# Two-layer trunk: another order of the value products, another place for the norm's products, and two-map buffers with a later combine in attention

## The chip, the cores and the metric

The kernel runs on one core of a Trainium2 chip. The metric is the device time of one execution in microseconds (us); lower is better. The core has a matrix engine (TensorE, PE in the profile, with its weight loads as PEld), VectorE (DVE), ScalarE (ACT), GpSimd (POOL), and a queue of DMA issues (SP). Each engine takes its instructions in a fixed order and waits for semaphores of the others.

## The reference, cut to what matters

The program has two layers over 1024 tokens of width 1024, in fp32. The first layer mixes tokens by a gated MLP and a gated delta rule, the second by differential attention; each layer then has an MLP and a gate with a second input ("PLE"). The change touches the second layer's value projection and attention:

```python
hn = rms_norm(h, ln_mix_o[i])
q, k, v = jnp.split(hn @ w_qkv_o[i], 3, axis=-1)
# 8 heads, two maps of 64 each; v: 8 heads of 128
q = rms_norm(q, q_gain) * 64 ** -0.5
k = rms_norm(k, k_gain)
logits = q @ k.T - slopes * dist          # for both maps, causal
probs = softmax(logits)
attn = probs[:, :, 0] - lam * probs[:, :, 1]
o = attn @ v
o = rms_norm(o, sub_gain) * (1.0 - lam_init)
```

with `rms_norm(h, g) = h * rsqrt(mean(h * h) + eps) * g` over the features of a token.

## The kernel before, in words

**Precision.** A matrix operand is held as a pair hi and lo of a reduced fp32 format, and a product of two operands is three passes of PE (`mm3`: hi·hi, hi·lo, lo·hi). `split` makes such a pair: a cast on ACT (L231) gives hi, a subtraction on DVE or POOL (L235) gives lo. Weights come from memory by DMA through a ring of raw tiles and a ring of split tiles (`w`).

**Hidden state.** `h` lies with features on the partitions, in two halves of 512 tokens: `acc[m][half]` is features 128m onward. `put_h` (L246, L247) makes the pair hi, lo of h times the norm's gain. The factor r, one over the root of the mean square of a token, is applied to a product's result and not to its operand. `add_square` (L258) sums the squares of a half into `sqs`, 128x512; `rms` adds those over the partitions with four 128x1 products against a column of ones (the trace counts them as eight), scales on DVE (L274), and takes the power on POOL (L276).

**The PLE gate** (`ple`) runs over the two halves. At the end of each half it calls `put_h` for its eight tiles, then `take_hs`, which calls `rms`. The last thing in it is therefore the second half's `rms`.

**The value projection** (`values`) comes next. It multiplies two by two blocks of 512 (a: tokens half and feature half; b: feature half and value column half) by a scheme of seven block products in place of eight, with sums of blocks as operands: s1 to s4 of tokens, t1 to t4 of weights. One block product (`product`) is 4 k-tiles by 4 banks by 3 passes = 48 passes of 128x512. There are two sets of four PSUM banks, x and y. The order in the text is a11·b11 into x, a12·b21 into y, s2·t2 into x (added to what is there), s1·t1 into y (new), s3·t3 into x, s4·b22 into y, a22·t4 into x. `copies` (ACT) takes a set out to SBUF, scaled by r; `close` takes a set out to the result, scaled and added to an earlier copy on DVE (L765), and without such a copy on ACT; `store` writes it to `v_dram`. The sums of tokens s1 to s4 overwrite `acc` (L738, L740).

**Attention** follows. It has 8 heads of 8 blocks of 128 queries. For a block, `logits(r)` of map r = 0, 1 multiplies q by the keys (two passes, qh and ql), DVE adds the bias and takes a running minimum (L1234), ACT takes the exponential with its sum (L1237). `combine` (L1243 to L1245) adds the second map, times a factor from both sums, to the first. `transpose` turns the combined block on PE and copies it out on ACT (L1255), `value` multiplies it by v (`po`, L1265). At step g the loop issues logits(0) of block g, the combine of g-1, the transpose of g-2, logits(1) of g and the value of g-2. `lg0` has three buffers in turn (two in A4, one in A5), `lg1` has one (the rest of A5).

Beside these steps `pump` feeds PE with the projections of q and k of the next head (256-wide passes), whose results leave by L1143 to L1152: a square on ACT, a reduction on DVE (L1145), an addition and a power on POOL (L1146, L1148), and two multiplications on DVE (L1152). `begin` turns k and q of the next head, with their copies on ACT and DVE (L1188, L1189 for `ks`; L1200 to L1202 for `qh` and `ql`), in the step of block 6, or 7 for the last; the second half of the keys follows at block 2 or 3. v is read from `v_dram` for two heads at a time, 1 MB each, into A0 and A1 in turn: two reads at the start, the others at steps 18 and 34.

**What sets the order.** A scheduler with a timeline of its own orders each engine's instructions. The class `Ordered` lets the program pin PE instructions behind others (`behind`, and `floor`, which holds all that follows behind a given product). PE's instructions carry L81 (products) and L84 (transposes). The lines named here and in the prediction are the kernel before's, unless it says otherwise; from L717 on the changed file's numbers differ by a few.

Of the kernel before, what the change touches and what calls it, by code (L numbers as in the profile page):

```python
# [18 lines left out]
P = 128  # L19
# [100 lines left out]
class Trunk:  # L120
# [144 lines left out]
    def rms(self, half, sqs, ms=None, rows=True, far=False):  # L265


        nc = self.nc
        if ms is None:
            pt = self.aux_ps()  # L270
            for t in range(4):
                self.pe.matmul(pt[:, t : t + 1], lhsT=sqs[:, t * P : (t + 1) * P], rhs=self.ones[:, 0:1], start=True, stop=True)
            ms = self.sp.tile([P, 4], F32, tag="ms", name=self.nm("ms"))
            nc.vector.tensor_scalar(ms, pt[:, 0:4], 1.0 / D, EPS, ALU.mult, ALU.add)  # L274
        r = self.sp.tile([P, 4], F32, tag=f"r{half}", name=self.nm("r"))
        nc.gpsimd.tensor_tensor(r, ms, self.mhalf[:, 0:4], ALU.pow)  # L276
# [12 lines left out]
        return r, rb  # L289
# [372 lines left out]
    def ple(self, pT, acc, wg, wpj, gain_next, h_dram):  # L662
# [19 lines left out]
        for h in range(2):  # L682
# [18 lines left out]
            self.take_hs(h, rows=False)  # L701

    def values(self, acc, gain, w_qkv):
# [7 lines left out]
        def tt(out, a, b, op):  # L713
            nc.vector.tensor_tensor(out, a, b, op)
            return out
# [42 lines left out]
        def close(i, l, ps, plus=None):  # L758
            for q in R:
                t = self.tmp()  # L760
                f = r[i][:, q : q + 1]
                if plus is None:
                    nc.scalar.activation(t, ps[q], AF.Copy, scale=f)
                else:
                    nc.vector.scalar_tensor_tensor(t, ps[q], f, plus[q], ALU.mult, ALU.add)  # L765
                store(i, l, q, t)

        b11 = right(lambda k: raw(0, 0, k))
        t1 = [self.slot(f"c{8 + k}", [P, HT], F32, "t1") for k in R]
        t2 = [self.slot(f"c{4 + k}", [P, HT], F32, "t2") for k in R]  # L770
        for k in R:
            tt(t1[k], raw(0, 1, k), raw(0, 0, k), ALU.subtract)
# [14 lines left out]
        s1, s2, s3, s4 = ([acc[m + k][h] for k in R] for m, h in ((4, 1), (0, 0), (0, 1), (4, 0)))  # L787
        for k in R:
            scaled(s3[k], k, 0, s3[k], ALU.subtract)
            scaled(s2[k], k, 0, s1[k], ALU.subtract)  # L790
        for k in R:
            scaled(s4[k], 4 + k, 0, s2[k], ALU.add)
        s2s = left(("A4", "A5"), s2)
        t2s = right(lambda k: t2[k])
# [3 lines left out]
        t1s = right(lambda k: t1[k])  # L798
        t = [self.slot(f"c{8 + k}", [P, HT], F32, "t") for k in R]
        product(y, s1s, t1s, True)  # L800
        copies(t, y, 1)

        def make_t3(k):
            b = raw(1, 1, k)
            return tt(b, b, raw(0, 1, k), ALU.subtract)
# [4 lines left out]
        close(1, 1, x, t)  # L810
        s4s = left(("A3", "A2"), s4)
# [288 lines left out]
    def attention(self, w_qkv, v_dram, w_out, gain_next, h_dram):  # L1100
# [107 lines left out]
        class Block:  # L1208


            def __init__(me, hd, b):
                me.hd, me.b, me.g = hd, b, len(blocks)
                me.n = (b + 1) * P
                me.lg = [lg0[len(blocks) % 3], lg1]
# [42 lines left out]
            def value(me):  # L1257
# [3 lines left out]
                o, v = os[hd], vs[hd // 2]  # L1261
                po = self.aux([P, P], "sc", "po")
                for k in range(b + 1):
                    self.pe.matmul(po, lhsT=me.aT[k // 4][:, (k % 4) * P : (k % 4 + 1) * P], rhs=v[:, k, (hd % 2) * P : (hd % 2 + 1) * P], start=k == 0, stop=k == b)
# [48 lines left out]
        qks, vs, os = [[] for _ in range(8)], [], [[] for _ in range(8)]  # L1313

        def values(pr):
            vs.append(self.slot(f"A{pr % 2}", [P, NT, 256], F32, "v"))
            nc.sync.dma_start(vs[pr], v_dram[:, :, pr * 256 : (pr + 1) * 256].rearrange("t p f -> p t f"))
# [41 lines left out]
        for g in range(8 * NB + 2):  # L1359
            if g in (2 * NB + 2, 4 * NB + 2):  # L1360
                values(g // (2 * NB) + 1)
# [4 lines left out]
            if 0 < g <= 8 * NB:  # L1366
                blocks[g - 1].combine()
# [978 lines left out]
```

## Time and profile before

| | |
|---|---|
| median of three runs | 2523.72 us (2525.03, 2522.82, 2523.72) |
| profiled execution | 2523.94 us, span 2522.2 us, granted clock 0.997 |
| up to 1188 us (first layer, up to the second half of its PLE gate) | PE busy 1185.57 of 1188.00 |
| 1188 to 1224, end of the gate and start of the value products | in the prediction |
| 1224 to 1291, the rest of the value products | PE busy 67.00 of 67.00, granted clock 0.98 |
| 1291 to 1308, projections ahead of the first head | PE busy 17.00 of 17.00 |
| 1308 to 1650, attention | in the prediction |
| 1650 to the end (output projection, MLP, gate) | PE busy 866.14 of 872.00 |

The granted clock is the share of full speed that PE was given. A row of the timeline has the start, the duration of one instruction or of the group from its first start to its last end, the engine, the line, out<-in and the count; in brackets stands the idle time of the engine before it and what ended that. A row of the waits has the waiting instruction, what released it, the sum in us, the count, and the longest.

### The profile page before, as it was taken

Reading aid. Unit: us, or ns where it says so; the run is one execution under the profiler, and the core shown is the slowest. Engines: PE = TensorE matmul, PEld = TensorE weight load, DVE = VectorE, ACT = ScalarE, POOL = GpSimd, SP = SyncE. Lnnn points to the kernel's source line nnn. Section 1 sums busy time; section 2 is a strip of 40 time slices with the busy share of each in tenths; the row PEclk is TensorE's granted clock in tenths of the full one; section 3 lists DMA queues with packets and bytes.
Section 4 is the critical chain, followed back from the end, with each engine's and each line's share of the span. In section 5 each row is a group of like instructions: output and inputs, shape, how many; then the busy total and the mean of one; then the engine's idle time right before and its main releaser. Section 6 shows DMA issues by size and latency. Waiting matters only on the chain.

```text
span 2522.2 us, 39013 instructions
## 1 busy us (share of the span) xinstructions
PE 2492.6 (99%) x13465; PEld 2114.7 (84%) x13465; DVE 1813.1 (72%) x3510; ACT 1346.0 (53%) x2732; POOL 245.6 (10%) x235
## 2 busy tenths in 40 slices
PE   9999999999999999999999999999999999999999
PEld 8898998888888888888799888988788888888887
DVE  7867664887666887556837777777887666787576
ACT  6635473655555445444536776765654555445452
POOL 0211220000000000000033433320000000000000
PEclk9999999999999999999999999999999999999999
DMA  8464445567558656554340211266467558656651
GB/s 240 126 181 112 149 127 164 163 207 250 177 172 281 216 179 201 180 159 139 117 142 27 68 43 59 89 205 223 149 214 240 178 177 282 209 185 203 198 174 65
DMA packets 322447, 420.46 MB, mean 167 GB/s; under 512 B 46692, under 2 KB 178760, under 8 KB 322248
## 3 DMA queue, kind: packets, MB, share of 16 engines
q1 hardware_dynamic: 321688, 417.43, 51.5%
q8 instruction: 106, 1.74, 0.3%
q14 instruction: 93, 0.76, 0.1%
q10 hardware_dynamic: 560, 0.53, 0.1%
HBM read 301.46 MB, written 116.40 MB: 166 GB/s over the span
## 4 chain that ended last, share of the span: by engine, by line
PE 92%; DVE 4%; ACT 2%; issue 1%; DMA 0%; POOL 0%; SPq 0%; DVEq 0%; ACTq 0%
PE mm L81 81%; PE po L81 2%; PE aux L81 2%; PE qk L81 2%; PE tr L84 2%; DVE lg L1234 1%; ACT lg L1237 1%; ACT qh L1201 0%; ACT qh L1200 0%; PE pks L81 0%; PE pkq L81 0%; PE pkk L81 0%; PE pvn L81 0%; PE pgm L81 0%; DVE w L235 0%
## 5 line engine op out<-in xcount | busy, mean ns | idle before, releaser
L231 ACT CAST w<-raw 128x512 fp32r<-128x512 f32 x582 | 357.2, 618 | 475.2 <-PE mm L81 431.9
L81 PE MATMUL mm<-g,w 128*128 128x512 f32 x2592 | 601.2, 394 | 0.0
L81 PEld LDWEIGHTS mm<-g,w 128*128 128x128 f32 x2592 | 486.7, 188 | 113.4
L81 PE MATMUL mm<-hi,w 128*128 128x512 f32 x1728 | 554.2, 395 | 0.0
L235 DVE TENSOR_TENSOR w<-raw,w 128x512 fp32r<-128x512 f32 (+1 forms) x550 | 376.0, 690 | 199.7 <-ACT w L231 191.3
L81 PE MATMUL mm<-w,hi 128*128 128x256 f32 (+2 forms) x2112 | 439.0, 303 | 4.8 <-DVE k L1152 4.8
L81 PEld LDWEIGHTS mm<-hi,w 128*128 128x128 f32 x1728 | 324.3, 188 | 74.0 <-DVE w L235 0.4
L81 PEld LDWEIGHTS mm<-w,hi 128*128 128x128 f32 x2112 | 338.4, 189 | 24.5 <-DVE k L1152 6.3
L81 PE MATMUL mm<-lo,w 128*128 128x512 f32 x864 | 340.2, 394 | 0.0
L81 PE MATMUL mm<-w,lo 128*128 128x256 f32 (+2 forms) x1056 | 317.4, 301 | 0.0
L81 PE MATMUL mm<-t,w 128*128 128x512 f32 x1152 | 271.5, 394 | 0.0
L81 PEld LDWEIGHTS mm<-t,w 128*128 128x128 f32 x1152 | 216.5, 188 | 50.7
L81 PEld LDWEIGHTS mm<-w,lo 128*128 128x128 f32 x1056 | 199.3, 189 | 8.0
L81 PEld LDWEIGHTS mm<-lo,w 128*128 128x128 f32 x864 | 162.4, 188 | 36.2
L276 POOL TENSOR_TENSOR r<-ms,mhalf 128x4 f32<-128x4 f32 x12 | 14.6, 1213 | 1554.3 <-DVE ms L274 1523.5
L235 DVE TENSOR_TENSOR g<-graw,g 128x512 fp32r<-128x512 f32 x216 | 147.7, 685 | 3.6 <-DMA gd<-g 3.5
L231 ACT CAST g<-graw 128x512 fp32r<-128x512 f32 x216 | 132.9, 618 | 19.4 <-DVE g L235 5.6
L1237 ACT ACTIVATE lg<-lg,nm 128x1024 f32<-128x1024 f32 (+7 forms) x128 | 99.5, 778 | 59.1 <-DVE nm L1234 58.6
L371 ACT ACTIVATE g<-g 128x512 f32<-128x512 f32 x100 | 63.1, 632 | 78.5 <-DVE g L305 78.1
L81 PE MATMUL mm<-ohi,w 128*128 128x512 f32 x256 | 85.0, 400 | 0.6 <-DVE acc L1452 0.3
L1234 DVE CUSTOM_DVE_ANT_0 lg<-qk,al 128x512 f32<-128x512 f32 (+3 forms) x128 | 74.1, 587 | 15.1 <-PE qk L81 12.0
L81 PE MATMUL mm<-ahi,w 128*128 128x512 f32 x256 | 83.1, 400 | 0.2 <-ACT ahi L1785 0.2
(373 smaller groups left out, 3673.4 us busy)
## 6 DMA issues: line engine op xcount, KB each, us to landing
raw<-in_w_mlp_dram SPq DMA_DIRECT2D x352, 256.0 KB, 3.2
graw<-gd SPq DMA_DIRECT2D x224, 256.0 KB, 2.7
gd<-g SPq DMA_DIRECT2D x192, 256.0 KB, 3.3
raw<-in_w_ple_gate_dram SPq DMA_DIRECT2D x76, 256.0 KB, 3.7
acc<-h_dram SPq DMA_DIRECT2D x64, 256.0 KB, 4.9
keep<-in_w_mlp_dram SPq DMA_DIRECT2D x64, 256.0 KB, 4.6
raw<-in_w_in_e_dram SPq DMA_DIRECT2D x60, 256.0 KB, 3.7
h_dram<-acc SPq DMA_DIRECT2D x48, 256.0 KB, 2.9
```

The lines of the kernel that those rows point to most:

```text
L81: self._next(self.engine.matmul(*a, **k))
L84: self._next(self.engine.transpose(*a, **k))
L231: inst = self.nc.scalar.copy(hi, src)
L235: inst = (lo_engine or self.nc.vector).tensor_tensor(lo, src, f32(hi), ALU.subtract)
L276: nc.gpsimd.tensor_tensor(r, ms, self.mhalf[:, 0:4], ALU.pow)
L371: nc.scalar.activation(g, src, AF.Relu)
L1234: nc.vector.tensor_tensor_reduce(out=lg[:, k0:k1], in0=ps[:, : k1 - k0], in1=al[:, u0 + k0 : u0 + k1], scale=-0.5 ** (hd + 1), scalar=3.0e ...
L1237: nc.scalar.activation(lg[:, :n], lg[:, :n], AF.Exp, bias=nm[:, r, nch - 1 : nch], scale=-1.0, accum_out=me.sums[:, b, r : r + 1])
```

## The change

**Value products.** The first product is now a12·b21, into y, copied out by ACT; the second a11·b11, into x, closed on DVE with that copy. Then come the second half's ones products of `rms`: `ple` calls `take_hs` for the first half only, `values` calls `rms` for the second with the bank `y[0]`, and `floor` holds its products behind the last product issued before it. The third product is a22·t4, which has no sum of tokens as operand; its result is copied to four tiles w. The four products with sums of tokens follow: s2·t2, s1·t1, s3·t3, s4·b22. s2 goes to tiles of its own (c0 to c3). All sixteen result tiles are closed on DVE; before, four of them were plain copies on ACT.

**Attention.** The three buffers each hold both maps (A4, A5, A1), so `lg1` turns through three as `lg0` does. The combine of block g-1 is issued after logits(1) of block g. With A1 taken, v has A0 alone, in two halves of 512 KB: a read for each head, at block 2 of the head before it (and two at the start).

```diff
-    def rms(self, half, sqs, ms=None, rows=True, far=False):
+    def rms(self, half, sqs, ms=None, rows=True, far=False, pt=None):
...
-            pt = self.aux_ps()
+            pt = self.aux_ps() if pt is None else pt
...
-            self.take_hs(h, rows=False)
-
+            if h == 0:
+                self.take_hs(0, rows=False)
+        self.hs[1] = self.hs_new[1]
...
-        b11 = right(lambda k: raw(0, 0, k))
+        b21 = right(lambda k: raw(1, 0, k))
...
-        product(x, a11, b11, True)
-        copies(u, x, 0)
-        b21 = right(lambda k: raw(1, 0, k))
-        for k in R:
-            tt(t2[k], t1[k], raw(1, 1, k), ALU.subtract)
-        product(y, a12, b21, True)
-        close(0, 0, y, u)
+        product(y, a12, b21, True)
+        copies(u, y, 0)
+        b11 = right(lambda k: raw(0, 0, k))
+        for k in R:
+            tt(t1[k], raw(1, 1, k), ALU.subtract, t2[k])
+        product(x, a11, b11, True)
+        close(0, 0, x, u)
+
+        self.pe.floor = self.pe.mark
+        r[1] = self.rms(1, self.sqs[1], rows=False, pt=y[0])[0]
+        self.pe.floor = None
...
+        t4s = right(lambda k: tt(raw(1, 0, k), t2[k]))
+        product(y, a22, t4s, True)
+        s2 = [scaled(self.slot(f"c{k}", [P, HT], F32, "s2"), k, 0, s1[k], ALU.subtract) for k in R]
+        s2s = left(("A4", "A5"), s2)
+        t2s = right(lambda k: t2[k])
...
+        copies(w, y, 1)
...
         product(x, s2s, t2s)
         copies(u, x, 0)
         s1s = left(("A0", "c"), s1)
         t1s = right(lambda k: t1[k])
+        product(y, s1s, t1s, True)
...
         close(1, 1, x, t)
+        close(1, 0, x, w)
         s4s = left(("A3", "A2"), s4)
         b22 = right(lambda k: raw(1, 1, k))
         product(y, s4s, b22)
         close(0, 1, y, u)
-        t4s = right(lambda k: tt(t2[k], t2[k], raw(1, 0, k), ALU.add))
-        product(x, a22, t4s)
-        close(1, 0, x)
...
-        lgs = [self.slot(f"A{4 + i}", [P, 2, S], F32, "lg") for i in range(2)]
-        lg0 = [lgs[0][:, 0], lgs[0][:, 1], lgs[1][:, 0]]
-        lg1 = lgs[1][:, 1]
+        lgs = [self.slot(t, [P, 2, S], F32, "lg") for t in ("A4", "A5", "A1")]
+        lg0, lg1 = ([x[:, r] for x in lgs] for r in range(2))
...
-                me.lg = [lg0[len(blocks) % 3], lg1]
+                me.lg = [lg0[len(blocks) % 3], lg1[len(blocks) % 3]]
...
-        def values(pr):
-            vs.append(self.slot(f"A{pr % 2}", [P, NT, 256], F32, "v"))
-            nc.sync.dma_start(vs[pr], v_dram[:, :, pr * 256 : (pr + 1) * 256].rearrange("t p f -> p t f"))
+        vs = self.slot("A0", [P, 2, NT, P], F32, "v")
+
+        def values(hd):
+            nc.sync.dma_start(vs[:, hd % 2], v_dram[:, :, hd * P : (hd + 1) * P].rearrange("t p f -> p t f"))
...
-            if g in (2 * NB + 2, 4 * NB + 2):
-                values(g // (2 * NB) + 1)
+            if g % NB == 2 and 0 < g // NB < 7:
+                values(g // NB + 1)
...
-            if 0 < g <= 8 * NB:
-                blocks[g - 1].combine()
             pump()
...
                 blocks[g].logits(1)
+            if 0 < g <= 8 * NB:
+                blocks[g - 1].combine()
             pump()
```

What stands where on an engine, before and after, at three places; the first is the seam between gate and value products, on two engines. In the rows a number behind a name tells one tile from another; an instruction that has a second row with 128x1 alone is the running minimum's write.

PE at the second half's ones products, first before (`mm` are the value products' banks, `w` the split weights, `hi` and `lo` the token operands, `aux` the ones' bank):

```order
L81 MATMUL mm_12293<-w_12352,lo_11737 128x512
L81 MATMUL mm_12293<-w_12358,hi_11740 128x512
L81 MATMUL mm_12293<-w_12359,hi_11740 128x512
L81 MATMUL mm_12293<-w_12358,lo_11741 128x512
L81 MATMUL aux_12224<-ones,sqs_11849 128x1 x4
L81 MATMUL mm_12287<-w_12236,hi_11720 128x512
L81 MATMUL mm_12287<-w_12237,hi_11720 128x512
```

The same place after (`mm_12281` is y's first bank, the one that the ones borrow; the other three of y and one of x are 12282 to 12284 and 12277; `s` is a part of s2):

```order
L81 MATMUL mm_12282<-w_12470,hi_12216 128x512
L81 MATMUL mm_12283<-w_12470,hi_12216 128x512
L81 MATMUL mm_12284<-w_12470,hi_12216 128x512
L81 MATMUL mm_12277<-w_12547,s_12537 128x512
L81 MATMUL mm_12281<-ones,sqs_11849 128x1 x4
L81 MATMUL mm_12282<-w_12471,hi_12216 128x512
L81 MATMUL mm_12282<-w_12470,lo_12217 128x512
```

Before, 54 of the value products stand ahead of the ones; after, 118 do, all of the first two block products and part of the third among them.

DVE at the last addition to `sqs`, before (`acc` are sums of tokens, `t` the PLE gate's, `s` and `w` lower parts of operands):

```order
L235 TENSOR_TENSOR s_12467<-acc_8285,s_12466 128x512
L740 SCALAR_TENSOR_TENSOR acc_8288<-acc_8288,cols,acc_8287 128x512
L740 SCALAR_TENSOR_TENSOR acc_8286<-acc_8286,cols,acc_8285 128x512
L235 TENSOR_TENSOR s_12467<-acc_8285,s_12466 128x512
L676 SCALAR_TENSOR_TENSOR acc_8288<-t_12185,acc_8288 128x512
L740 SCALAR_TENSOR_TENSOR acc_8287<-acc_8285,cols,acc_8287 128x512
L740 SCALAR_TENSOR_TENSOR acc_8285<-acc_8285,cols,acc_8288 128x512
L258 TENSOR_TENSOR sqs_11849<-sqs_11849,t_12189 128x512
```

And after (`raw` are the sums of weights for t4, `u` the copy of the first product):

```order
L716 TENSOR_TENSOR raw_12735<-raw_12735,raw_12737 128x512
L676 SCALAR_TENSOR_TENSOR acc_8288<-t_12185,acc_8288 128x512
L742 SCALAR_TENSOR_TENSOR s_2552_12533<-acc_8285,cols,acc_8288 128x512
L742 SCALAR_TENSOR_TENSOR acc_8287<-acc_8285,cols,acc_8287 128x512
L716 TENSOR_TENSOR raw_12744<-raw_12744,raw_12746 128x512
L763 SCALAR_TENSOR_TENSOR t_12425<-mm_12277,r_11759,u_12285 128x512
L742 SCALAR_TENSOR_TENSOR acc_8286<-acc_8286,cols,s_2552_12533 128x512
L258 TENSOR_TENSOR sqs_11849<-sqs_11849,t_12189 128x512
L247 SCALAR_TENSOR_TENSOR lo_12221<-acc_8288,cols,hi_12220 128x512
```

The sums for t4 and the first close (L763 of the changed file) now stand ahead of that addition. From the first `lo` of the second half on (L247), 30 instructions stand ahead of it before, 39 after.

The second place is DVE at the turn from the third head to the fourth, before, from the reciprocal to the second copy of the new keys (`ks` the keys, `lg` a block's maps, `rs` the factor of the combine, `ss` the reduction for q and k, `ql` the low part of q, `ISA` the minimum pass):

```order
L1243 RECIPROCAL rs_15084<-sums_14498 128x1
L1234 ISA lg_12933,nm_15074<-qk_15079,al_12917,nm_15074 128x512
L1234 ISA nm_15074 128x1
L1244 SCALAR_TENSOR_TENSOR rs_15084<-sums_14498,nlam,rs_15084 128x1
L1189 SCALAR_TENSOR_TENSOR ks_15054<-tr_15055,kg,ks_15054 64x512
L1245 SCALAR_TENSOR_TENSOR lg_12932<-lg_12933,rs_15084,lg_12932 128x896
L1145 TENSOR_REDUCE ss_15135<-t_15133 128x8
L1202 SCALAR_TENSOR_TENSOR ql_12928<-tr_15064,qg,qh_15067 64x256
L1234 ISA lg_12933,nm_15074<-qk_15112,al_12917 128x512
L1234 ISA nm_15074 128x1
L1274 RECIPROCAL c_3111_15324<-sums_14498 128x4
L1189 SCALAR_TENSOR_TENSOR ks_15054<-tr_15055,kg,ks_15054 64x512
```

And after, from the combine's second instruction to the same copy (L1249 is the wide combine, L1193 the copy of the keys):

```order
L1248 SCALAR_TENSOR_TENSOR rs_15128<-sums_14510,nlam,rs_15128 128x1
L1249 SCALAR_TENSOR_TENSOR lg_12944<-lg_12944,rs_15128 128x896
L1238 ISA lg_12945,nm_15085<-qk_15086,al_12928 128x512
L1238 ISA nm_15085 128x1
L1193 SCALAR_TENSOR_TENSOR ks_15065<-tr_15066,kg,ks_15065 64x512
L1238 ISA lg_12945,nm_15085<-qk_15119,al_12928 128x512
L1238 ISA nm_15085 128x1
L1150 TENSOR_REDUCE ss_15146<-t_15144 128x8
L1238 ISA lg_12945,nm_15085<-qk_15090,al_12928,nm_15085 128x512
L1238 ISA nm_15085 128x1
L1206 SCALAR_TENSOR_TENSOR ql_12939<-tr_15075,qg,qh_15078 64x256
L1193 SCALAR_TENSOR_TENSOR ks_15065<-tr_15066,kg,ks_15065 64x512
```

Before, the first copy of the keys stands ahead of the wide combine (128x896); after, it stands behind it and behind a minimum pass more.

The third place is DVE within the fourth head, where q and k leave their bank, before:

```order
L1145 TENSOR_REDUCE ss_15307<-t_15305 128x8
L1234 ISA lg_12933,nm_15333<-qk_15378,al_12917 128x384
L1234 ISA nm_15333 128x1
L1234 ISA lg_12933,nm_15333<-qk_15334,al_12917 128x384
L1234 ISA nm_15333 128x1
L1234 ISA lg_12932,nm_15401<-qk_15402,al_12917 128x512
L1234 ISA nm_15401 128x1
L1265 COPY o_15044<-po_15312 128x128
L1243 RECIPROCAL rs_15407<-sums_15163 128x1
L1152 TENSOR_TENSOR q_15301<-mm_15175,ssf_15310 128x256
L1152 TENSOR_TENSOR k_15303<-mm_15175,ssf_15310 128x256
```

And after:

```order
L1206 SCALAR_TENSOR_TENSOR ql_12940<-tr_15267,qg,qh_15270 64x256
L1150 TENSOR_REDUCE ss_15318<-t_15316 128x8
L1206 SCALAR_TENSOR_TENSOR ql_12940<-tr_15267,qg,qh_15270 64x256
L1238 ISA lg_12945,nm_15345<-qk_15346,al_12928 128x384
L1238 ISA nm_15345 128x1
L1157 TENSOR_TENSOR q_15312<-mm_15182,ssf_15321 128x256
L1157 TENSOR_TENSOR k_15314<-mm_15182,ssf_15321 128x256
```

Before, three minimum passes (L1234) and two small instructions stand between the reduction (L1145) and the two multiplications (L1152); after, one pass and a `ql` do.

More of the change, by code (lines that the diff above doesn't have):

```diff
@@ L711, in values, with tt @@
         v_dram = self.dp.tile([NT, P, D], F32, name="v_dram")
-        def tt(out, a, b, op):
+        def tt(a, b, op=ALU.add, out=None):
+            out = a if out is None else out
             nc.vector.tensor_tensor(out, a, b, op)
@@ L756, in store, with close @@
             nc.sync.dma_start(v_dram[4 * i + q, :, l * HT : (l + 1) * HT], t)
-        def close(i, l, ps, plus=None):
+        def close(i, l, ps, plus):
             for q in R:
                 t = self.tmp()
[L761 to L765, printed above, removed]
+                nc.vector.scalar_tensor_tensor(t, ps[q], r[i][:, q : q + 1], plus[q], ALU.mult, ALU.add)
                 store(i, l, q, t)
-        b11 = right(lambda k: raw(0, 0, k))
+        b21 = right(lambda k: raw(1, 0, k))
         t1 = [self.slot(f"c{8 + k}", [P, HT], F32, "t1") for k in R]
@@ L771, in values @@
         for k in R:
-            tt(t1[k], raw(0, 1, k), raw(0, 0, k), ALU.subtract)
+            tt(raw(0, 1, k), raw(0, 0, k), ALU.subtract, t1[k])
         x, y = banks(), banks()
@@ L786, in values @@
             scaled(acc[4 + k][1], 4 + k, 1, acc[k][1], ALU.add)
-        s1, s2, s3, s4 = ([acc[m + k][h] for k in R] for m, h in ((4, 1), (0, 0), (0, 1), (4, 0)))
+        s1, s3, s4 = ([acc[m + k][h] for k in R] for m, h in ((4, 1), (0, 1), (4, 0)))
+        t4s = right(lambda k: tt(raw(1, 0, k), t2[k]))
[3 more added lines that the diff above has]
+        t2s = right(lambda k: t2[k])
+        w = [self.sp.tile([P, HT], F32, tag=n, name=self.nm("w"), bufs=1) for n in ("rb1", "sqs0", "sqs1")]
+        w.append(self.slot("c4", [P, HT], F32, "w"))
+        copies(w, y, 1)
+        for k in R:
+            scaled(s4[k], 4 + k, 0, s2[k], ALU.add)
         for k in R:
             scaled(s3[k], k, 0, s3[k], ALU.subtract)
[L790 to L794, printed above, removed]
         product(x, s2s, t2s)
@@ L804, in make_t3 @@
             b = raw(1, 1, k)
-            return tt(b, b, raw(0, 1, k), ALU.subtract)
+            return tt(b, raw(0, 1, k), ALU.subtract)
         s3s = left(("A4", "A5"), s3)
@@ L1311, in attention @@
         waiting = []
[L1313 to L1317 removed]
+        qks, os = [[] for _ in range(8)], [[] for _ in range(8)]
+        vs = self.slot("A0", [P, 2, NT, P], F32, "v")
+        def values(hd):
+            nc.sync.dma_start(vs[:, hd % 2], v_dram[:, :, hd * P : (hd + 1) * P].rearrange("t p f -> p t f"))
         fill = self.stream([proj_qk(hd, qks[hd]) for hd in range(8)])
```

5 lines of the change are left out of this document (2 added, 3 removed).

## The prediction

> **What bounds the kernel now.** I read the head of the page first, then the engines stage by stage, and the waits of TensorE last.
>
> ```profile
> span 2522.2 us, 39013 instructions
> PE 2492.6 (99%) x13465; PEld 2114.7 (84%) x13465; DVE 1813.1 (72%) x3510; ACT 1346.0 (53%) x2732; POOL 245.6 (10%) x235
> ```
>
> TensorE (PE) is busy for 99% of the span. The number of products does not change, so what is left to win is the 29.6 us in which it is idle, and whatever it does at a lower clock. The stages say where that is (span, then busy us of PE, PEld, DVE, ACT, POOL, then the granted clock):
>
> ```profile
> 1188.00:1224.00 36.00, 29.80 (x128) 24.18 (x127) 32.76 (x52) 17.13 (x29) 0.00 (x0) 0.95 0.51 157
> 1308.00:1650.00 342.00, 327.08 (x2535) 309.47 (x2534) 254.06 (x746) 244.54 (x611) 129.66 (x130) 0.99 0.18 59
> ```
>
> The first is the seam between the PLE gate and the value products: 6.2 us idle. The second is attention: 342.00 - 327.08 = 14.9 us idle. Both are places that the change touches. The waits of PE name the releasers; the first row is from the window 1188 to 1291, the others from 1308 to 1650.
>
> ```profile
> PE aux L81 <- DVE sqs L258: 6.2, 1, 6.2
> PE tr L84 <- DVE ks L1189: 5.0, 4, 1.2
> PE mm L81 <- DVE k L1152: 4.8, 8, 1.2
> PE qk L81 <- ACT qh L1201: 1.3, 2, 0.9
> PE qk L81 <- DVE nm L1234: 1.2, 5, 0.5
> DVE rs L1243 <- ACT lg L1237: 29.1, 30, 1.8
> ```
>
> One wait of 6.2 us stands alone; those of attention are many and none is over 1.2 us. The last row is no wait of PE: it is DVE standing before the combine until the exponential of the second map is done, 29.1 us in all.
>
> **The change, part one: the value products.** In the timeline of PE the seam reads:
>
> ```profile
> 1202.84 0.63 PE L81 MATMUL mm<-w,hi 128*128 128x512 f32 x2
> ...
> 1215.12 0.39 PE L81 MATMUL mm<-w,lo 128*128 128x512 f32 x1
> 1221.71 1.87 PE L81 MATMUL aux<-ones,sqs 128*128 128x1 f32 x8 [6.20 <-DVE sqs L258]
> 1223.44 1.20 PE L81 MATMUL mm<-w,hi 128*128 128x512 f32 x2
> 1224.44 0.63 PE L81 MATMUL mm<-w,lo 128*128 128x512 f32 x1
> 1224.86 1.05 PE L81 MATMUL mm<-w,hi 128*128 128x512 f32 x2
> 1225.72 0.63 PE L81 MATMUL mm<-w,lo 128*128 128x512 f32 x1
> 1226.14 1.05 PE L81 MATMUL mm<-w,hi 128*128 128x512 f32 x2
> 1227.00 0.51 PE L81 MATMUL mm<-w,lo 128*128 128x512 f32 x1
> 1227.35 0.62 PE L81 MATMUL mm<-w,hi 128*128 128x512 f32 x2
> ...
> 1234.96 44.59 PE L81 MATMUL mm<-w,s 128*128 128x512 f32 x192
> ...
> 1290.48 0.40 PE L81 MATMUL mm<-w,hi 128*128 128x256 f32 x2
> ```
>
> A product takes 44.59 / 192 = 0.232 us from start to start. The wait costs three things. The gap: 1215.12 to 1221.71 is 6.59 from start to start where 0.23 would do, 6.36 lost. The norm's own eight passes take 1.73 (to 1223.44); the same eight elsewhere take 0.81:
>
> ```profile
> 2423.40 0.95 PE L81 MATMUL aux<-ones,sqs 128*128 128x1 f32 x8
> 2424.21 0.47 PE L81 MATMUL mm<-w,hi 128*128 128x512 f32 x1
> ```
>
> so 0.92 more is lost. Then nine products take 3.91 (1223.44 to 1227.35) instead of 9 x 0.232 = 2.09: 1.82 lost. That this is at a lower clock shows in the stage
>
> ```profile
> 1222.00:1228.00 6.00, 6.00 (x20) 5.10 (x20) 5.96 (x13) 2.38 (x4) 1.50 (x1) 0.56 0.08 13
> ```
>
> with a granted clock of 0.56. Sum 9.10. The other way round: the stage lasts 1290.48 - 1202.84 = 87.64; 7 x 48 = 336 products and the eight passes need 336 x 0.232 + 0.81 = 78.8, which leaves 8.8. I take 8.9.
>
> The Trainium skill, "TensorE: Matmul & The Clock Gate", section Part 1: The HAM clock gate, says that an idle window of about 3.4 us halves the PE clock and that about 3.4 us of activity restores it. The row agrees (0.56 after a gap of 6.2). By that rule a shorter wait than 3.4 us would cost its own length only, which matters for a rival below.
>
> Does the gap close? Ahead of the norm's passes PE's order now has 118 products instead of 54, so it gets there at 1202.84 + 118 x 0.232 = 1230.2 instead of 1215.4. The sum that it waits for is DVE's last add to sqs:
>
> ```profile
> 1201.28 2.07 DVE L247 SCALAR_TENSOR_TENSOR lo<-acc,cols,hi 128x512 fp32r<-128x512 f32 x3
> ...
> 1220.97 0.68 DVE L258 TENSOR_TENSOR sqs<-sqs,t 128x512 f32<-128x512 f32 x1
> ```
>
> From the end of the first lo (about 1201.9) to that add, DVE runs 30 instructions in 19.0 us without a pause, 0.634 each. Its new order has 39 there (the four sums for t4, a close of the first quarter and others are drawn forward), so the add starts at 1201.9 + 39 x 0.634 = 1226.7 and ends near 1227.4: 2.8 us ahead of PE. Two places beside this could turn tight. Ahead of the sum stands the first close of a product (L763), which needs the 83rd product done: PE is past it at 1202.84 + 83 x 0.232 = 1222.1, DVE comes at about 1225, so it doesn't wait. And the third product's first bank is the one that the norm borrows, so its twelve products stand last, up to the 168th; the 159th frees an operand buffer, and between that and the 185th, which writes the bank again, ACT has eight instructions to do (seven casts, and the copy of that bank). 25 x 0.232 = 5.8 us are there. Eight by the cast's row
>
> ```profile
> L231 ACT CAST w<-raw 128x512 fp32r<-128x512 f32 x582 | 357.2, 618 | 475.2 <-PE mm L81 431.9
> ```
>
> are 8 x 0.62 = 5.0 us: ready by 0.8 us, the tightest place that I find. The four closes that ACT did for the last product are now DVE's,
>
> ```profile
> 1233.23 2.72 DVE L765 SCALAR_TENSOR_TENSOR t<-mm,r,u 128x512 f32<-128x512 f32 x4
> ```
>
> 2.7 us beside the 11 us of the product that follows, so they cost nothing; without that cover they would cost 2.7. Value taken: -8.9. Its bounds are -9.1 and, with a new wait of 3 us that still lowers the clock (0.92 + 1.82 again), -8.9 + 5.7 = -3.2.
>
> **Part two: attention.** The combine of a block waits for the second map's exponential. With one buffer for that map DVE had to run it before the next block's second logits; now it comes behind them. No operation is added or made cheaper, and DVE is not the bound there (254.06 of 342). So the gain is what PE's waits shrink by, at most the 14.9 us of idle time. I worked through one head by DVE's new order, at the two kinds of wait that cost most. At a head's turn the timeline has
>
> ```profile
> 1455.85 0.16 DVE L1243 RECIPROCAL rs<-sums 128x1 f32<-128x1 f32 x1 [1.06 <-ACT lg L1237]
> ...
> 1457.61 1.15 DVE L1245 SCALAR_TENSOR_TENSOR lg<-lg,rs,lg 128x896 f32<-128x896 f32 x1
> ...
> 1459.67 0.68 DVE L1234 CUSTOM_DVE_ANT_0 lg<-qk,al 128x512 f32<-128x512 f32 x1
> ...
> 1460.47 0.76 DVE L1189 SCALAR_TENSOR_TENSOR ks<-tr,kg,ks 64x512 fp32r<-64x512 f32 x1
> ...
> 1461.37 0.63 PE L84 MATMUL tr<-ident,lg 128*128 128x128 f32 x4 [1.25 <-DVE ks L1189]
> ```
>
> PE's transposes wait until the second ks has left their bank, 5.4 us after the reciprocal (1455.85 to 1461.23). The new order puts the wide combine ahead of the first ks, where before it came between the two, and one logits pass more ahead of the second. On the way to the second that is 0.68 and one small copy more, some 6.4 us; in return one logits pass fewer stands before the exponential that the reciprocal waits for, which so comes about 0.65 earlier. Net some 0.3 us worse at each of 7 turns: +2. With the combine's place and the pass both counted in full and nothing earlier it would be 1.15 + 0.68 = 1.83 a turn, 7 x 1.83 = +12.8, the upper bound. Within a head the other wait is
>
> ```profile
> 1478.28 1.64 POOL L1148 TENSOR_TENSOR ssf<-ss,mhalf 128x8 f32<-128x8 f32 x1
> ...
> 1480.51 0.41 DVE L1152 TENSOR_TENSOR k<-mm,ssf 128x256 f32<-128x256 f32 x1
> ...
> 1480.97 0.51 PE L81 MATMUL mm<-w,hi 128*128 128x256 f32 x2 [0.56 <-DVE k L1152]
> ```
>
> PE needs the bank that q and k leave. Before, three logits passes stood between the reduction (L1145) and them; now one pass and a short ql do. POOL's power ends at 1479.92, so they gain 0.3, and 0.5 more because the reduction itself stands one instruction earlier: the 0.56 goes. Of the 4.8 us under this name I let 3.5 go. Sum for attention: +2 - 3.5 = -1.5, between -12.3 (the four waits of PE named above gone) and +12.8.
>
> The value rows are now read a head at a time, eight loads in place of
>
> ```profile
> v<-v_dram SPq DMA_DIRECT2D x4, 1024.0 KB, 5.2
> ```
>
> that land in 5.2 us in the median. Each is issued six of a head's eight blocks before its head starts. Two of the old ones, two heads apart, stand at
>
> ```profile
> 1427.29 0.37 SPq L1317 DMA_DIRECT2D v<-v_dram  x1
> ...
> 1530.26 0.37 SPq L1317 DMA_DIRECT2D v<-v_dram  x1
> ```
>
> so a head takes 51.5 us and six blocks some 38: a landing of 5 us is covered, and costs nothing.
>
> **Sum.** The profiled execution took 2523.94 us, its span and 1.7 around it, 0.2 above the median of the three runs. 2523.9 - 8.9 - 1.5 = 2513.5.
>
> **The rivals.** First, attention opens up: the 29.1 us that DVE stood before the combine are used, and two thirds of the 14.9 us of idle time go. 2523.9 - 8.9 - 10 = 2505.0. For it speaks that PE's waits there name DVE for 11 of 12.3 us; against it that a wait's last link is often ACT or POOL, as with the power above.
>
> Second, the gap moves instead of closing: the last add to sqs comes 6 us later than reckoned, since it now stands behind operands that wait for weights from memory. From 2.8 us late on PE waits; at 3 us of wait the time is 2523.9 - 3.2 = 2520.7 and, with attention as it was, no measurable change. By the Trainium skill's rule such a wait, being under 3.4 us, would leave the clock alone, and the time would be 2518; no run so far shows it.
>
> Third, attention gives back what the value products win: waits of 0.6 to 1.4 us at the seven turns, 4 to 10 us in all, for 2519 to 2525. For it speaks the order at the turn; against it the exponential's earlier start.
>
> Fourth, on the other side: the wide combine holds the first ks at every turn by the full 1.83, and at the second half of each head's keys the combine of 384 (0.6 by the ratio of widths) does so too: 12.8 + 8 x 0.6 = 17.6, for 2523.9 - 8.9 + 17.6 = 2532.6. It decides from the point at which DVE's way to the second ks grows by more than the exponential comes earlier (0.65).
>
> **How the numbers follow.** A measurement of this kernel can tell about 0.2%, 5 us, from no change. Forecast (2510 to 2518) 0.58; attention opens up 0.16; the gap moves 0.07; attention gives back 0.13; slower 0.06. So faster 0.74, within 0.2% 0.20, slower 0.06. The range 2504 to 2521 takes the forecast, most of the first rival and the near half of the second and third, some 0.8.
>
> **What would show it.** In the changed kernel's profile the row of PE's wait for sqs (L258) is gone or under 1 us; the granted clock is 1.00 through the seam; from the first value product to the first 256-wide product pass about 78.8 us. In attention PE's wait for k shrinks from 4.8 to under 2, that for ks grows from 5.0 by up to 2, and the idle time of the stage is 11 to 15 us. I am wrong in part one if a wait of over 2 us stands anywhere in the value products, and in part two if the idle time of attention changes by more than 5 us either way.

## The result: 0.2% slower, and where the gain went

The changed kernel takes 2528.41 us in the median of 20 runs (2526.23 to 2533.79), the kernel before 2523.94 in 20 runs beside it: a ratio of 1.0019, interval 1.0012 to 1.0026. Forecast were 2513.5 and a range of 2504 to 2521. The profiled execution took 2528.24 us. Of the runs below, one execution of e8 took 5576.81 us; it is left out of e8's row, whose profile is that of a further execution of the same kernel (e8b, 2525.03 us). The head of the changed kernel's page:

```profile
span 2526.5 us, 38990 instructions
PE 2492.5 (99%) x13465; PEld 2119.9 (84%) x13465; DVE 1818.5 (72%) x3514; ACT 1345.6 (53%) x2732; POOL 245.4 (10%) x235
```

Three places in PE's timeline cut the program into the same pieces in every kernel: the first 256-wide pass (it ends the value products), the last value product of attention (`po`), and the products `aux<-ident,r` of the norm behind the output projection. The first of before stands in the prediction; the others are

```profile
1748.10 1.95 PE L81 MATMUL po<-v,aT 128*128 128x128 f32 x16
1777.39 1.16 PE L81 MATMUL aux<-ident,r 128*128 128x128 f32 x8 [0.93 <-POOL r L276]
```

and after the change

```profile
1281.37 0.40 PE L81 MATMUL mm<-w,hi 128*128 128x256 f32 x2
1746.40 1.06 PE L81 MATMUL po<-v,aT 128*128 128x128 f32 x8
1782.68 1.16 PE L81 MATMUL aux<-ident,r 128*128 128x128 f32 x8 [0.95 <-POOL r L276]
```

The windows between them (length, then PE's busy time; the number ahead of the last two is the granted clock), before and after:

```profile
1290.48:1750.05 459.57, 444.17 (x3238) 412.08 (x3237) 330.77 (x938) 307.85 (x757) 150.71 (x150) 0.99 0.30 99
1750.05:1777.39 27.34, 25.77 (x115) 19.65 (x113) 21.80 (x39) 13.19 (x24) 3.63 (x4) 1.00 0.78 257
```

```profile
1281.37:1747.46 466.09, 446.12 (x3244) 417.45 (x3243) 335.76 (x943) 310.34 (x756) 150.49 (x150) 0.98 0.31 98
1747.46:1782.68 35.22, 26.72 (x108) 20.66 (x108) 21.83 (x39) 12.60 (x23) 3.63 (x4) 0.85 0.61 201
```

Up to the first place the change is 9.11 us ahead (1290.48 - 1281.37). The stretch of attention is 6.52 longer (466.09 - 459.57): PE is idle for 4.57 more and busy for 1.95 more. The end, from attention's last value product to the norm, which the prediction did not treat, is 7.88 longer (35.22 - 27.34), of which 6.93 is idle time. That is 5.29 behind; the rest of the program gives 0.99 back, to the 4.3 between the spans.

**The value products** went as reckoned. In PE's timeline and DVE's:

```profile
1202.74 0.63 PE L81 MATMUL mm<-w,hi 128*128 128x512 f32 x2
...
1230.05 0.95 PE L81 MATMUL mm<-ones,sqs 128*128 128x1 f32 x8
```

```profile
1226.30 0.67 DVE L258 TENSOR_TENSOR sqs<-sqs,t 128x512 f32<-128x512 f32 x1
```

```profile
1202.84:1224.00 21.16, 21.16 (x93) 17.20 (x92) 21.16 (x35) 9.89 (x19) 0.00 (x0) 1.00 0.45 133
1222.00:1228.00 6.00, 6.00 (x28) 4.86 (x27) 6.00 (x10) 3.62 (x7) 0.00 (x0) 1.00 0.72 236
```

The sum is ready at 1226.97, PE gets to it at 1230.05; there is no idle time and no lowered clock, and the products take 1281.37 - 1202.74 = 78.63 us.

**Attention and the end.** PE's waits in the changed kernel, and behind them one of the kernel before that the prediction does not show:

```profile
PE tr L84 <- ACT aT L1259: 8.0, 5, 1.8
PE mm L81 <- DVE acc L1456: 7.4, 1, 7.4
PE qk L81 <- DVE nm L1238: 7.2, 9, 1.4
PE tr L84 <- DVE ks L1193: 2.6, 5, 0.6
PE mm L81 <- DVE k L1157: 0.2, 1, 0.2
```

```profile
PE tr L84 <- ACT aT L1255: 0.6, 1, 0.6
```

The waits for ks and k, which the prediction worked on, fell from 9.8 to 2.8. Two others rose: for the minimum pass (`nm`), from 1.2 to 7.2, and for the transposes' copy (`aT`), from 0.6 to 8.0. The turn from the fourth head to the fifth shows the first. DVE, ACT, POOL and PE:

```profile
1495.61 0.60 DVE L1238 CUSTOM_DVE_ANT_0 lg<-qk,al,nm 128x384 f32<-128x384 f32 x1
...
1497.43 0.16 DVE L1247 RECIPROCAL rs<-sums 128x1 f32<-128x1 f32 x1 [1.12 <-ACT lg L1241]
...
1497.94 1.82 DVE L1249 SCALAR_TENSOR_TENSOR lg<-lg,rs 128x896 f32<-128x896 f32 x1
1499.69 0.68 DVE L1238 CUSTOM_DVE_ANT_0 lg<-qk,al 128x512 f32<-128x512 f32 x1
1500.41 0.75 DVE L1193 SCALAR_TENSOR_TENSOR ks<-tr,kg,ks 64x512 fp32r<-64x512 f32 x1
```

```profile
1496.26 1.05 ACT L1241 ACTIVATE lg<-lg,nm 128x896 f32<-128x896 f32 x1 [3.73 <-DVE nm L1238]
...
1497.75 1.07 POOL L1285 TENSOR_TENSOR o<-o,of 128x512 f32<-128x512 f32 x1
```

```profile
1500.43 0.50 PE L81 MATMUL qk<-ks,qh 128*128 128x512 f32 x1 [0.46 <-DVE nm L1238]
...
1503.30 0.30 PE L81 MATMUL qk<-ks,qh 128*128 128x128 f32 x1 [1.43 <-DVE nm L1238]
...
1504.47 0.63 PE L84 MATMUL tr<-ident,lg 128*128 128x128 f32 x4 [0.55 <-DVE ks L1193]
```

DVE stands from 1496.3 to 1497.4, since its next instruction, the reciprocal of the combine, waits for ACT's exponential, which ends at 1497.3. Then it runs the wide combine until 1499.76. The minimum passes of block 7 stand behind that, and PE has no free bank for its logits. Before, the combine stood behind two of these passes at this turn. The combine takes 1.82 here; three of the eight of this width do, and five take 1.15. Then the clock falls:

```profile
1500.00:1506.00 6.00, 3.29 (x17) 2.35 (x17) 5.87 (x17) 3.51 (x7) 1.83 (x2) 0.98 0.00 0
1505.80:1509.30 3.50, 3.40 (x16) 3.40 (x17) 2.41 (x7) 2.09 (x6) 0.00 (x0) 0.52 0.00 0
```

This is not the only turn with a low clock. In the change's attention the granted clock is 0.50 in four stretches, each behind a turn (1451.2 to 1454.5, 1505.8 to 1509.1, 1557.0 to 1563.7, 1611.7 to 1614.9); before, it is so in two (1462.8 to 1466.1, 1565.2 to 1568.5).

The waits for `aT` are not at the turn's minimum passes. All five stand some 15 us behind a turn. This one is at the transposes of the old head's last block:

```profile
1519.77 0.59 ACT L1259 COPY aT<-tr 128x512 f32<-128x512 f32 x1
```

```profile
1520.41 0.65 PE L84 MATMUL tr<-ident,lg 128*128 128x128 f32 x4 [1.61 <-ACT aT L1259]
```

PE has turned the first half of that block at 1517.85 and needs the copy of it (`aT`) before the second half. ACT makes that copy behind two copies of q (`qh`) and the square of a projection. Before, the copy stood ahead of the square (1526.42 and 1527.30), and PE had other products between the two halves.

At the end, SP, DVE and PE, and last the same place on PE before:

```profile
1750.41 2.22 SPq L1444 DMA_DIRECT2D acc<-h_dram  x5
```

```profile
SPq L1444 <- DMA h_dram<-res: 8.4, 3, 4.4
```

```profile
1756.00 0.69 DVE L1456 TENSOR_TENSOR acc<-acc,mm 128x512 f32<-128x512 f32 x1 [6.73 <-DMA acc<-h_dram]
```

```profile
1756.74 0.79 PE L81 MATMUL mm<-ohi,w 128*128 128x512 f32 x1 [7.41 <-DVE acc L1456]
```

```profile
1753.71 0.50 PE L81 MATMUL mm<-ohi,w 128*128 128x512 f32 x1 [0.31 <-DVE acc L1452]
```

The output projection adds its products to residual tiles that are read back into A0 (features 0 to 511) and A1. Before, A0 was free after the sixth head, and its four tiles were read from 1666 on. Now A0 holds v until the last value product; its loads go out at 1750.41, behind a load that waits for a store (loads into `acc` wait so three times here, 8.4 us in all), and PE stands still for 7.41 us. The clock is 0.50 from 1751.6 to 1761.7, during that wait and after it.

### The profile page after: what moved, and what is told of

It is laid out like the page before. It is cut to its first block, busy times and chain, and to the rows that moved or that the text cites. A ratio compares the mean times of both kernels' runs of the same rounds, so it can differ in the third digit from the quotient of the medians.

```text
span 2526.5 us, 38990 instructions
## 1 busy us (share of the span) xinstructions
PE 2492.5 (99%) x13465; PEld 2119.9 (84%) x13465; DVE 1818.5 (72%) x3514; ACT 1345.6 (53%) x2732; POOL 245.4 (10%) x235
## 4 chain that ended last, share of the span: by engine, by line
PE 95%; DVE 3%; DMA 1%; ACT 1%; issue 1%; POOL 0%; SPq 0%; DVEq 0%; POOLq 0%; ACTq 0%
PE mm L81 82%; PE po L81 3%; PE qk L81 2%; PE aux L81 2%; PE tr L84 2%; DVE lg L1238 1%; DMA h_dram<-res 0%; DVE lg L1249 0%; PE aux L84 0%; PE pks L81 0%; PE pkq L81 0%; PE pkk L81 0%; PE pvn L81 0%; PE pgm L81 0%; PE pab L84 0%
## 5 line engine op out<-in xcount | busy, mean ns | idle before, releaser
L235 DVE TENSOR_TENSOR w<-raw,w 128x512 fp32r<-128x512 f32 x554 | 376.6, 687 | 195.7 <-ACT w L231 180.7
L1241 ACT ACTIVATE lg<-lg,nm 128x128 f32<-128x128 f32 (+7 forms) x128 | 99.2, 776 | 51.8 <-DVE nm L1238 51.5
```

The source lines that it names most:

```text
L235: inst = (lo_engine or self.nc.vector).tensor_tensor(lo, src, f32(hi), ALU.subtract)
L1241: nc.scalar.activation(lg[:, :n], lg[:, :n], AF.Exp, bias=nm[:, r, nch - 1 : nch], scale=-1.0, accum_out=me.sums[:, b, r : r + 1])
```

## The experiments

Theory A: three separate causes, as above. Each ratio is to the kernel before on the same chip, from 4 to 11 executions of the experiment. "Attention" and "end" are the two windows above, cut at the same three rows of each run's own profile. They are those of one execution: the executions of one kernel differ by up to 8 us (the change: 2526.23 to 2533.79), so a difference of a few us between two windows counts only where the medians agree with it.

| kernel | us, median | ratio to before, interval | attention | end |
|---|---|---|---|---|
| before | 2523.94 | | 459.57 | 27.34 |
| after | 2528.41 | 1.0019 (1.0012, 1.0026) | 466.09 | 35.22 |
| e1 value part alone | 2515.55 | 0.9968 (0.9956, 0.9981) | 465.05 | 27.31 |
| e2 attention part alone | 2539.17 | 1.0059 (1.0047, 1.0072) | 468.23 | 33.07 |
| e3 A0 and A1 exchanged | 2531.13 | 1.0030 (1.0018, 1.0041) | 466.34 | 34.37 |
| e5 the same, combine's line back | 2531.86 | 1.0030 (1.0019, 1.0041) | 467.58 | 34.43 |
| e6 one buffer for the second map | 2520.07 | 0.9982 (0.9973, 0.9991) | 459.32 | 33.52 |
| e7 combine pinned at the turns | 2511.49 | 0.9953 (0.9941, 0.9966) | 452.00 | 33.38 |
| e8 e3 and the queue's order | 2526.61 | 1.0011 (1.0002, 1.0020) | 466.44 | 29.09 |
| e9 e3, e7 and e8 together | 2507.24 | 0.9933 (0.9921, 0.9946) | 452.16 | 27.32 |
| e12 o scaled on ACT | 2507.31 | 0.9935 (0.9919, 0.9952) | 449.21 | 29.81 |
| e15 e12, combine forced ahead | 2517.46 | 0.9977 (0.9967, 0.9986) | 459.12 | 32.21 |
| e14 e9 and e12 together | 2501.91 | 0.9911 (0.9897, 0.9925) | 447.50 | 26.50 |

**e1 and e2: each part alone** (the diff's pieces in `rms`, `ple` and `values`, and those in `attention`).

> The kernel before with the value products' part of the change alone (order of the products, place of the norm's ones). Theory A (three separate causes: value products -9.1 us, attention +6.5 by its last value product, output projection +7): 2523.9 - 9.1 = 2514.8, every landmark from the first 256-wide product to the end 9.1 earlier. Rival C (the value part disturbs attention, by what it leaves in the queues or by when attention starts): 2519 or more, with attention longer than before.

> The kernel before with attention's part of the change alone. Theory A: 2528.4 + 9.1 = 2537.5, with the wait of 7.4 us for acc in the output projection. Rival C: 2530 or less, since without the value part the loss in attention is not there.

The parts come to -8.4 and +15.2, together +6.8 where the whole change is +4.5; the intervals of both parts, some 3 us either way, cover the 2.3 between. Rival C falls: attention's part loses without the value part. (e2's wait for acc is 5.9 us, not 7.4.) The profiled execution of e1 is its slowest (2519.50). Its attention is 5.5 us longer than before, with a wait for k of 2.9 us in the first head and a low clock after it, which the profile of the whole change does not show; the median does not have this loss.

**e3 and e5: A0 against A1, and the line of the combine.**

```diff
-        lgs = [self.slot(t, [P, 2, S], F32, "lg") for t in ("A4", "A5", "A1")]
+        lgs = [self.slot(t, [P, 2, S], F32, "lg") for t in ("A4", "A5", "A0")]
-        vs = self.slot("A0", [P, 2, NT, P], F32, "v")
+        vs = self.slot("A1", [P, 2, NT, P], F32, "v")
```

> The changed kernel with the places A0 and A1 exchanged: the third two-map buffer in A0, v in A1. Theory A: the residual tiles that the output projection adds first lie in A0, which v holds to its last product; with v in A1 they can load from the last combined block's transposes on, the 7.4 us wait and the slow products behind it go: 2521 to 2522. Rival B (the wait is that of a DMA queue that is late as a whole because attention ends otherwise): the wait stays at 4 us or more, 2525 to 2528.

> As the exchange of A0 and A1, and the combine of the block before put back ahead of the second logits; the three two-map buffers and v by head stay. Theory A, with the later combine as attention's whole loss: attention is as long as before within 1 us, 2515. Rival D (the loss is from v read by head, or from the buffers): 2521 to 2522 as with the exchange alone.

Both of my expectations failed, and the rivals' times did not come either. The exchange alone wins nothing: PE's wait for acc is 4.3 instead of 7.4 us, the end 0.85 shorter, and the whole not faster. And the combine's line has no weight: with it back in its old place, DVE's order differs from e3's in one exchange of two neighbours and PE's in nothing. The scheduler places the combine; what it has lost is the obligation, from the single buffer, to run it before the next second map is written.

**e6: one buffer for the second map, v still by head in A0.**

```diff
-                me.lg = [lg0[len(blocks) % 3], lg1[len(blocks) % 3]]
+                me.lg = [lg0[len(blocks) % 3], lg1[0]]
```

with the combine ahead of the second logits again, which one buffer needs.

> The changed kernel with one buffer for the second map again, and the combine ahead of the second logits; v by head in A0 stays. Theory A (the loss inside attention comes from the order that the scheduler makes once the second map has three buffers; v by head costs only at the end, where A0 is held): attention as short as in the kernel with the value part alone, PE's waits for nm under 2 us and for aT under 1, then a wait of 4 to 7 us for acc after the last value product: 2519.5 to 2522.5. Rival D (v by head disturbs attention): the waits for nm and aT of 7 and 8 us stay, 2526 or more.

PE's instructions come out in the same order as in e1. Its waits:

```profile
PE tr L84 <- DVE ks L1193: 5.0, 4, 1.2
PE mm L81 <- DVE k L1157: 4.9, 8, 1.2
PE mm L81 <- DVE acc L1456: 3.6, 1, 3.6
PE qk L81 <- DVE nm L1238: 1.1, 5, 0.5
PE tr L84 <- ACT aT L1259: 0.6, 1, 0.6
```

Attention is as before (459.32 against 459.57), so the buffers and the order that they permit are its loss; v by head is not. The end keeps 6.2 us of loss (33.52 - 27.31), with a wait for acc of 3.6 us where 4 to 7 were expected; the whole is 4.5 us longer than e1 (2520.07 - 2515.55).

**e7, e8 and e9: the two orders set by hand.** e7 keeps the buffers and holds, on DVE, the combine of block 6 behind the first copy of the next head's keys (`behind` sets an order only):

```diff
-                nc.vector.reciprocal(rs, sums[:, b, 1:2])
+                inst = nc.vector.reciprocal(rs, sums[:, b, 1:2])
+                if b == 6 and (me.hd + 1, 0) in turn:
+                    self.pe.behind(inst, turn[me.hd + 1, 0])
```

(`turn` keeps the name of that copy.) e8 is e3 with the half-1 residual tile of m = 7 held behind the four loads of A1 in SP's queue; e9 has all.

> The changed kernel with the combine of each head's block 6 pinned behind the first copy of the next head's keys, on DVE. Theory A (at a turn the wide combine stands ahead of the minimum passes that free the logits' banks and of the keys' copy): PE's waits for nm fall from 7.2 to under 3 us and each turn gets 1 to 3 us shorter, 2522 to 2525. Rival E (the loss is spread over the order as a whole): within 2 us of 2528.4 or slower.

> The exchange of A0 and A1, and the last residual load of the second half put behind the four of A1 in the DMA queue. Theory F (the end's wait is that of loads which stand in the queue behind one that waits for a store to land): A1's loads are issued some 2.5 us earlier and PE's wait for acc falls from 4.3 to under 2 us: 3 to 5 us less than with the exchange alone, 2526 to 2528. Rival B (the loads would be late anyway, since v leaves A1 with the last product): within 1 us of 2531.

> The two edits together with the exchange: combine pinned at the turns, the DMA queue's order. By theories A and F the sum of both: 2520 to 2523; if the value part's 8.4 us then is all that shows against the kernel before, attention's part is worth nothing; below 2515 it would beat the value part alone.

The pin gains 16.9 us, far more than the 3 to 6 expected: attention falls to 452.00, 7.6 below before. PE's waits for nm and aT go, while those for qh and k come to 2.9 and 2.2; in e7

```profile
PE qk L81 <- DVE nm L1240: 1.7, 2, 1.1
PE tr L84 <- ACT aT L1263: 0.8, 2, 0.7
```

and the same turn on DVE in e9, which has e7's order of instructions on PE, DVE, ACT and POOL, is

```profile
1494.31 0.69 DVE L1240 CUSTOM_DVE_ANT_0 lg<-qk,al 128x512 f32<-128x512 f32 x1 [0.82 <-PE qk L81]
...
1495.04 0.74 DVE L1193 SCALAR_TENSOR_TENSOR ks<-tr,kg,ks 64x512 fp32r<-64x512 f32 x1
...
1499.85 1.15 DVE L1253 SCALAR_TENSOR_TENSOR lg<-lg,rs 128x896 f32<-128x896 f32 x1
```

The minimum pass comes as soon as its logits are there; the combine has moved behind all of block 7's passes. The clock stays up, in e7 too:

```profile
1281.77:1733.93 452.16, 440.59 (x3238) 408.84 (x3237) 333.13 (x942) 307.78 (x755) 148.91 (x150) 1.00 0.31 100
```

PE's idle time there is 11.57 (452.16 - 440.59), against 19.97 in the change and 15.40 before; its busy time is 440.59 against 446.12 and 444.17. So rival E falls: one pin at the turns brings back more than the loss. But the pin also gave other orders to PE and ACT after the turn, where the waits for `aT` were, and no run separates the two.

e7 and e9 have the same order of instructions in SP's queue as well, and differ in which of A0 and A1 holds v. So 4.25 us (2511.49 - 2507.24), and 6.1 of the end, are what v in A0 costs. The end's time needs both, the tile and the queue: e8 is 4.5 us below e3 (2531.13 - 2526.61). e9 is far below the 2520 to 2523 expected of it, and 8.3 us below the value part alone (2515.55, the intervals lie apart): with these orders attention's part is a gain. e8b, the further execution of e8, has 1.3 us of wait for acc:

> The exchange with the DMA queue's order, once more, for its profile: by theory F PE's wait for acc at the end is under 2 us (4.3 with the exchange alone) and the stretch from the last value product to the output projection's norm is 30 us or less (34.7 with the exchange alone, 27.6 before).

**e12, e15 and e14: the 1.82 us combine.** e12 takes POOL's multiplication away from over it:

```diff
-                nc.gpsimd.tensor_tensor(o[hf], o[hf], f.unsqueeze(2).to_broadcast([P, 4, P]), ALU.mult)
+                for t in range(4):
+                    nc.scalar.activation(o[hf][:, t], o[hf][:, t], AF.Copy, scale=f[:, t : t + 1])
```

> The changed kernel with the scaling of o (one 128x512 multiplication on POOL per half head) done by four 128x128 copies with a scale on ACT. Theory G (DVE's 128x896 combine takes 1.82 instead of 1.15 us where it overlaps that multiplication on POOL): no 896-wide combine over 1.2 us is left, and any combine over 1.2 times the usual of its width still overlaps a subtraction (L235) or another wide operation on POOL. In time 3 x 0.67 = 2 us less at most, 2526 to 2528, with 3 us either way for ACT's other order. Rival H (1.82 comes from the exponential that has just been written, or from ACT's copies beside it): some 1.82 stay at the turns of heads 2 to 4.

All eight wide combines take 1.15 or 1.16. But the time falls by 21 us, not 2. The scheduler now makes another order: from the fourth to the seventh head it puts the combine behind two to four of block 7's four passes by itself.

```profile
1548.20 0.75 DVE L1238 CUSTOM_DVE_ANT_0 lg<-qk,al,nm 128x512 f32<-128x512 f32 x1
...
1548.88 1.15 DVE L1249 SCALAR_TENSOR_TENSOR lg<-lg,rs 128x896 f32<-128x896 f32 x1
```

e15 forces it ahead of them again, for the second to the sixth head, by `behind` on block 7's first minimum pass:

> The scaling of o on ACT (as in the run before that took 2507.3), with the combine of block 6 pinned ahead of block 7's first minimum pass for heads 1 to 5, where DVE's order there had put it behind several passes for heads 3 to 6. No POOL work over it, so the combine stays 1.15. If the order at the turn is what costs (theory A): 2 to 4 us more for each of the three or four turns that change, PE's waits for nm back over 5 us, 2514 to 2520. If the overlap with POOL's multiplication is what costs (theory G): within 3 us of 2507.

```profile
1499.06 1.15 DVE L1251 SCALAR_TENSOR_TENSOR lg<-lg,rs 128x896 f32<-128x896 f32 x1
1500.13 0.68 DVE L1238 CUSTOM_DVE_ANT_0 lg<-qk,al 128x512 f32<-128x512 f32 x1
```

Without any overlap the order alone costs some 9.9 us of attention (459.12 - 449.21); the whole is 10.2 longer in the median (2517.46 - 2507.31). PE's waits for nm rise from 2.1 to 5.0, the least that was expected, so only part of it is that wait; those for aT stay small (3.0 and 2.7). Of the 9.9 PE is idle for 4.4 and busy for 5.6 (442.88 against 437.32). The other 7.0 us of the change's attention (466.09 - 459.12) are the overlap and the rest of its order; no run separates these.

> All that helped so far in one: the changed kernel with A0 and A1 exchanged, the DMA queue's order, o scaled on ACT, and the combine pinned behind the keys' first copy. If the order at the turn and the end's loads are all that was lost: the end of the second kernel with pins (27.6 us from the last value product to the norm) and attention as short as with o on ACT, 2503 to 2507; slower than 2507 if the pin forbids an order that the scheduler finds by itself.

e14 is the fastest: 0.9911 of before, at 2501.91 a little below the 2503 to 2507 expected.

## Why the prediction was wrong, step by step

- **Value products, -8.9: right.** 9.11 in the profile, 8.4 in e1's median. The arrival of PE (1230.2 reckoned, 1230.05), the sum's start (1226.7, 1226.30) and the 78.8 us (78.63) all held, and the clock stayed at 1.00. The copies' tight place held too.
- **A head's turn, +2: the first step that failed.** The prediction followed DVE only to the second copy of the keys. That wait even fell, from 5.0 to 2.6. It did not follow the minimum passes that free the logits' banks, though its order showed the combine ahead of them: PE's waits for nm rose from 1.2 to 7.2. Its premise that the combine "comes behind" the second logits failed too: the scheduler put it ahead of block 7's.
- **Within a head, -3.5 of the wait for k: right in kind, small in size, and not the whole.** That wait fell by 4.6, from 4.8 to 0.2. But the transposes' wait for aT, which had no term, rose by 7.4, from 0.6 to 8.0. That its cause is the order on ACT and PE is read from the rows; no run changed this order alone.
- **Only the idle time was priced.** Behind the turns the clock falls to half, in four stretches instead of two. Attention's PE is idle 4.6 us longer, and 2 of the 6.5 us lost are busy time.
- **"A landing of 5 us is covered, and costs nothing": the second step that failed.** The landing was covered. What was not looked at is who needs A0 next: 7.88 us at the end had no term and no rival. The runs put 6.1 of it down to v in A0 (e7 against e9).
- The third rival (attention gives back, 2519 to 2525) had the sign at 0.13, the fourth named the combine at the turn but charged it to the keys. The sum had -1.5 for attention, and 6.5 were measured; that is inside the bounds of -12.3 to +12.8. Without the 7.88 us of the end the time would have been 2520.5, just inside the range.

## What to carry to other kernels

A further buffer removes a wait and also the order that the wait enforced: in the new order, follow every bank and tile that the freed engine releases, not the one whose wait was the largest. When a tile gets a longer life, look up who takes its place next, and what stands ahead of that load in the queue. If a gain is lost to the order, a pin that sets only the order of one instruction can tell it, and here it turned 0.2% slower into 0.5% faster.

## What the hardware showed that was not expected

DVE's 128x896 combine takes 1.82 us where it begins 0.19 after POOL's 128x512 multiplication of `o` (1497.75 and 1497.94), and 1.15 elsewhere; with that multiplication on ACT all eight take 1.15 or 1.16. Not all work on POOL does this: the combine at 1392.9, which begins during POOL's 128x4 power (`of`), takes 1.15. The Trainium skill, "SBUF — State Buffer", section Who interferes with whom, says that a DVE instruction with two inputs in SBUF contends with a GpSimd instruction that reads SBUF, and that the order of issue decides which of them is held. The rows agree: the later one, DVE, loses 0.67 (1.82 - 1.15), a little less than the 0.88 that POOL still ran (1497.75 + 1.07 - 1497.94).

The granted clock fell to half behind a turn where no wait of PE was longer than 1.43 us, after 6 us in which it was busy for 3.29. It did so behind four turns of the change; in the 3.2 or 3.3 us ahead of each, PE was busy for 1.51 to 1.75. The Trainium skill, "TensorE: Matmul & The Clock Gate", section Part 1: The HAM clock gate, speaks of an idle window of about 3.4 us; its section A second HAM failure mode: psum-queue depth-cycling tells of short gaps that bring the clock down as well. The trace agrees with the second: several short waits close together cost more than their length. The prediction's reading of the first, that a shorter wait than such a window costs its own length only, does not hold here.
